# One layer of a gated HGRN2 / Mamba-2 hybrid: thirteen more pairs of projections as Strassen products, in a stage of their own

## The chip, the cores and the metric

The kernel runs on one core of a Trainium2 chip. A core has a matrix engine (PE), a vector engine (DVE), an activation engine (ACT), GpSimd (POOL), and queues on SP and POOL that start transfers between HBM and the on-chip memory. The metric is device microseconds (us) of one execution; shown are the median of several executions and, for one of them, a profile. In the rows L87 is line 87 of the kernel, and `out<-in` names the tiles that an instruction writes and reads.

## The reference, cut to what matters

1024 prompt tokens and 8 single-token samples go through one layer, 1032 columns in all. From the normed input `h` one projection gives everything:

```python
proj = h @ p['w_in']
q, f, i, og, z, xbc, dt, ga, gb = jnp.split(proj, IN_OFFSETS, axis=-1)
...
o_hg, S_new = _hgrn2_recurrence(qh, kh, vh, lh, S_hg)               # 8 heads of 128
o_hg = _rmsnorm(o_hg, p['hg_norm']) * jax.nn.silu(og)               # norm per head, gate og
...
y, h_new = _ssd_recurrence(xh * dtv, la, Bm, Cm, h_ssm)             # 8 groups, 4 heads of 64 each
y = y + p['d_skip'] * xh
y = y * jax.nn.silu(z)                                              # gate z
y = _rmsnorm(y.reshape(Bsz, T, SSM_GROUPS, 256), p['ssm_norm'])     # norm per group
u = jax.nn.sigmoid(ga + bma) * (o_hg @ p['w_br_a']) + jax.nn.sigmoid(gb + bmb) * (y @ p['w_br_b'])
x = x + g1 * (u @ p['w_out'])
x = x + g2 * (jnp.square(jax.nn.relu(h2 @ p['w_up'])) @ p['w_down'])
```

Neither recurrence reads `og`, `z`, `ga` or `gb`; these four enter behind the recurrences.

## The kernel before

Activations lie transposed: a plane is 128 channels by 1032 columns, and `h` is eight planes, each split into a rounded high part and the rest (`hh`, `hl`), as are all weights (`load_w`, L52 to L56). A **dense block** (`dense`, `dense_split`, L87) makes one output plane from eight input planes: three column parts of 344, eight planes, three products high/low, so 72 matmuls of 128x344.

A **Strassen pair** (`strassen_pair`, L1177) makes two output planes at once from halves of the columns and of the inputs: 7 products x 2 quarters x 4 planes x 3 = 168 matmuls of 128x258, in the order 1, 7, 6, 2, 5, 4, 3. It needs sums and differences of the input planes (`strassen_planes`), built once, and of the two weights (`strassen_weights`), built for every pair by ACT (L1133, L1138, L1141, L1145) and DVE (L1123, L1135) into two buffers that are handed on from product to product: the weights of product 1 of the next pair can be made only when product 4 of this one is through, and product 3 runs meanwhile. `keep` and `evac` take the results from the banks. In the kernel before, only `w_up` uses it, for 13 pairs.

The stages follow each other: HGRN2 (`phase_hgrn`; a head has dense blocks for f, i, q, og, and its recurrence follows), two gate blocks, `dt_phase`, eight SSM groups (`ssm_group`: blocks z, z, then B, C, x, x with their convolution, then the recurrence, the gate z and the norm), with the other gate blocks between and behind the groups, then `phase_merge` (`w_br_a`, `w_br_b`), `phase_out`, `phase_ffn`. Gated heads, groups and gate logits go through DRAM (`od`, `yd`, `gd`).

What sets the order: the program is written block after block; a scheduler then orders each engine's instructions, may fill a wait with later work, and prefers what stands under `high_priority`. Beside that, `beside` and `tick` lay a generator's steps between the matmuls of the dense blocks: a `yield n` asks for n matmuls before the next step. HGRN2's recurrence runs this way (`hgrn_head` returns the generator `hgrn_recurrence`); the SSM recurrence is straight code. Each engine works strictly in its order, so one waiting instruction holds all behind it. Weights and most planes are loaded by the SP queue, the stores of `w_up`'s results by the POOL queue.

The norms over channels are column sums on PE: `ones_sum` splits the squares into two parts and multiplies them by a 128x128 matrix of ones (L186, L187), three times for each head and each group; `rstd_from` follows on ACT and DVE over 128 partitions.

## Time and profile before

| | |
|---|---|
| median of 3 runs | 2526.72 us (2524.09 to 2531.59) |
| the profiled execution | 2523.55 us; its span 2521.7 us |
| PE busy | 2482.5 us, 98% |
| DVE, ACT, POOL busy | 1636.7, 1021.3, 70.2 us |
| moved by DMA | 301.14 MB, mean 119 GB/s |
| granted PE clock | 0.995 |

The span goes from the first to the last instruction; the execution's own time is 1.85 us more. A matmul's busy time overlaps with that of the next, so what a stream of matmuls costs is read from the stretch it fills over its count, not from its mean duration. A row of groups ends with the busy time, the mean of one instruction, and the idle time just before them with what ended it. In this execution the HGRN2 heads take 64 us each, to about 587 us; the SSM groups run from about 604 us to 1457 us with their gate blocks, the merge and output stages to 1871 us, the Strassen pairs of `w_up` from 1871 to 2133 us, and `w_down` to the end.

### The profile page before, as it was taken

What the parts mean: (1) busy time and instruction counts of PE and PEld (TensorE: products, weight loads), DVE (VectorE), ACT (ScalarE), POOL (GpSimd) and SP (SyncE); (2) the same over time, 40 slices, a digit from 0 to 9 for tenths busy, and PEclk for the clock granted to TensorE, in tenths of its full rate; (3) what the DMA queues carried; (4) which work ended last, traced back from release to release, by engine and by line L of the source; (5) the groups of instructions that cost most, each with busy time, mean ns of one, the idle gap of its engine ahead of it and who ended that gap; (6) DMA issues with size and microseconds to landing.
All of it is one profiled execution on the core that took longest, in us unless ns stands there. A gap on an engine that the chain in (4) does not pass through costs nothing.

```text
span 2521.7 us, 50588 instructions
## 1 busy us (share of the span) xinstructions
PE 2482.5 (98%) x21486; PEld 2427.6 (96%) x21486; DVE 1636.7 (65%) x3186; ACT 1021.3 (40%) x1569; POOL 70.2 (3%) x138
## 2 busy tenths in 40 slices
PE   8999999999999999999999999999999999999997
PEld 7999999999999999999999999999999999899997
DVE  7566666655677687787887844357976666443356
ACT  4444444445443544535535533124533334221123
POOL 0000000000000000000000000000012222000000
PEclk9999999999999999999999999999999999999999
DMA  6322223333334243243343554224233325232134
GB/s 256 119 103 88 101 103 103 103 105 94 102 111 135 86 145 127 94 146 126 102 145 111 187 188 147 72 102 142 98 108 104 104 101 193 102 110 93 67 106 146
DMA packets 103267, 301.14 MB, mean 119 GB/s; under 512 B 19057, under 2 KB 26033, under 8 KB 103025
## 3 DMA queue, kind: packets, MB, share of 16 engines
q1 hardware_dynamic: 96352, 279.99, 32.8%
q0 software_dynamic: 6256, 17.57, 2.0%
q8 instruction: 168, 2.75, 0.5%
q14 instruction: 59, 0.48, 0.1%
q10 hardware_dynamic: 432, 0.35, 0.0%
HBM read 241.02 MB, written 57.10 MB: 118 GB/s over the span
## 4 chain that ended last, share of the span: by engine, by line
PE 90%; DVE 3%; issue 3%; DMA 2%; ACT 1%; POOL 1%; SPq 0%; DVEq 0%; POOLq 0%; ACTq 0%
PE acc L87 69%; PE b L1177 7%; PE acc L139 2%; PE lv_ps L589 2%; PE y_ps L862 1%; PE yi_ps L866 1%; PE kvx_ps L826 1%; PE o_ps L561 1%; POOL ad L1203 1%; PE kv_ps L543 1%; PE ada_ps L225 1%; PE xt_ps L814 1%; PE cb_ps L796 1%; DMA vb<-vd 1%; DVE wl L56 0%
## 5 line engine op out<-in xcount | busy, mean ns | idle before, releaser
L87 PE MATMUL acc<-hl,wh 128*128 128x344 f32 x2232 | 725.0, 325 | 0.0
L87 PE MATMUL acc<-hh,wl 128*128 128x344 f32 x2232 | 718.3, 322 | 0.0
L87 PE MATMUL acc<-hh,wh 128*128 128x344 f32 x2232 | 715.6, 321 | 0.0
L87 PEld LDWEIGHTS acc<-hl,wh 128*128 128x128 f32 x2232 | 419.4, 188 | 4.3 <-issue 1.4
L87 PEld LDWEIGHTS acc<-hh,wl 128*128 128x128 f32 x2232 | 419.7, 188 | 1.5 <-issue 1.4
L87 PEld LDWEIGHTS acc<-hh,wh 128*128 128x128 f32 x2232 | 419.6, 188 | 0.1
L87 PE MATMUL acc<-hi,wl 128*128 128x344 f32 x1224 | 391.6, 320 | 1.3 <-DVE wl L56 1.3
L87 PE MATMUL acc<-lo,wh 128*128 128x344 f32 x1224 | 391.2, 320 | 1.4 <-ACT wh L54 1.4
L87 PE MATMUL acc<-hi,wh 128*128 128x344 f32 x1224 | 391.2, 320 | 0.0
L56 DVE TENSOR_TENSOR wl<-wr,wh 128x1024 fp32r<-128x1024 f32 x198 | 242.2, 1224 | 203.8 <-ACT wh L54 202.4
L54 ACT ACTIVATE wh<-wr 128x1024 fp32r<-128x1024 f32 x198 | 208.9, 1056 | 397.7 <-PE acc L87 325.7
L87 PEld LDWEIGHTS acc<-hi,wl 128*128 128x128 f32 x1224 | 230.1, 188 | 2.1 <-DVE wl L56 1.9
L87 PEld LDWEIGHTS acc<-lo,wh 128*128 128x128 f32 x1224 | 229.9, 188 | 2.0 <-ACT wh L54 2.0
L87 PEld LDWEIGHTS acc<-hi,wh 128*128 128x128 f32 x1224 | 230.2, 188 | 0.2
L1011 DVE SCALAR_TENSOR_TENSOR x<-acc,modT,x 128x344 f32<-128x344 f32 (+1 forms) x120 | 68.6, 572 | 187.8 <-PE acc L87 187.1
L746 DVE SCALAR_TENSOR_TENSOR cv<-raw,cst,cv 128x1024 f32<-128x1024 f32 x96 | 122.6, 1278 | 0.0
L1177 PE MATMUL b<-tl,wh 128*128 128x258 f32 x416 | 117.6, 283 | 0.0
L1177 PE MATMUL b<-th,wl 128*128 128x258 f32 x416 | 117.6, 283 | 0.0
L1177 PE MATMUL b<-th,wh 128*128 128x258 f32 x416 | 117.5, 283 | 0.0
L1203 POOL DMA_DIRECT2D ad<-r x122 | 65.9, 541 | 1491.5 <-DVE nrm_t L171 1227.8
L738 ACT ACTIVATE raw<-acc 128x344 f32<-128x344 f32 x96 | 43.0, 456 | 120.9 <-PE acc L87 120.4
L1177 PE MATMUL b<-h2h,wh 128*128 128x258 f32 x312 | 88.1, 283 | 0.0
(278 smaller groups left out, 4245.8 us busy)
## 6 DMA issues: line engine op xcount, KB each, us to landing
wr<-w_ssm SPq DMA_DIRECT2D x48, 512.0 KB
wr<-w_down SPq DMA_DIRECT2D x48, 512.0 KB
wr<-w_ada SPq DMA_DIRECT2D x36, 512.0 KB
lo<-ad SPq DMA_DIRECT2D x32, 516.0 KB
wr<-w_hg SPq DMA_DIRECT2D x32, 512.0 KB
w<-cumd SPq DMA_DIRECT2D x32, 512.0 KB
wr<-w_up SPq DMA_DIRECT2D x32, 512.0 KB
ad<-r POOLq DMA_DIRECT2D x104, 129.0 KB, 2.3
```

The source lines that it names most:

```text
L54: nc.scalar.activation(wh, wr, AF.Copy)
L56: nc.vector.tensor_tensor(wl, wr, wh.bitcast(F32), op=ALU.subtract)
L87: last = nc.tensor.matmul(acc[:M, :SW], a[:, sl], b[:, cs(s)], start=(i == 0 and j == 0), stop=(i == n - 1 and j == 2))
L139: k.nc.tensor.matmul(ac[s][:, :SW], a[:, sl], b[:, cs(s)], start=(i == 0 and j == 0), stop=(i == self.n - 1 and j == 2))
L225: nc.tensor.matmul(ps[r, :64], k.scT[:, i, :], w[:, :, r], start=i == 0, stop=i == KD - 1, tile_position=(0, 32 * g))
L543: nc.tensor.matmul(ps[:, c * P:(c + 1) * P], ktok[:, cc], vtok[:, cc], start=True, stop=True)
L589: nc.tensor.matmul(out, QK[hf][:, HT + key:HT + key + 32], x, start=True, stop=True, tile_position=(0, 32 * g))
L738: dense(k, w, k.hX, lambda s, ps: nc.scalar.activation(raw[:, 3 + s * SW:3 + (s + 1) * SW], ps, AF.Copy))
L746: nc.vector.scalar_tensor_tensor(cv[:, :T], raw[:, j:j + T], cw[:, j:j + 1], cv[:, :T], ALU.mult, ALU.add)
L1011: nc.vector.scalar_tensor_tensor(dst[:, :n], ps[:, :n], gate[:, 0:1], base[:, :n], ALU.mult, ALU.add)
L1177: nc.tensor.matmul(acc, a[:, sl], x[:, cols], start=(p in (1, 7, 2) and i == 0 and j == 0), stop=(i == KD // 2 - 1 and j == 2), skip_group ...
L1203: return r, lambda: nc.gpsimd.dma_start(ad[j][:, cols], r)
```

## The change

Blocks og (8), z (16) and two gate logits leave the HGRN2 and SSM stages. Behind the last SSM group a new stage, `phase_late`, builds the sums and differences of `h` while three gate blocks run, then makes 13 Strassen pairs in the order og, z, z, four times, and a pair of gates; one plain gate block ends it. HGRN2 stores its heads ungated and without norm, with the reciprocal root as one row (`rh`); the SSM stores its groups ungated. In the new stage the POOL queue brings them back; beside the next pair they are gated (`og_post`, `z_post`), the group norm is made there and applied one pair later, and POOL stores them again.

Norms: `row_rstd` multiplies the unsplit fp32 squares by 32 columns of ones, the three column parts into three 32-partition strips; the root runs over 96 partitions once; three rows go to DRAM and come back broadcast.

The SSM recurrence becomes a generator laid between the dense blocks of the next group (or the gate blocks) by `beside`. In it the subtraction and clipping in front of the exponential go from DVE (L849) to ACT (`Relu`), and the samples' part of the convolution becomes one instruction instead of three. HGRN2's decode work and the `w_ada` pairs are placed among the steps of the recurrence. `tick` is now also called by `strassen_pair` and `DenseK`.

```diff
-    nc.scalar.activation(a, ss, AF.Identity, bias=k.c_eps, scale=scale)
+    nc.scalar.activation(a, ss, AF.Identity, bias=k.c_eps[:a.shape[0]], scale=scale)
...
-    og = plane("og", "D")
-    dense(k, w[hd * 4 + 1], k.hX, copy_to(og))
-    tables(k, ((og, og, AF.Silu), (q, q, AF.Silu)))
-    return hgrn_recurrence(k, hd, f, F, dec, be, kd8, q, og, st, vb, vtok)
...
+    tables(k, ((q, q, AF.Silu),))
+    return hgrn_recurrence(k, hd, f, F, dec, be, kd8, q, st, vb, vtok)
...
+    nc.sync.dma_start(k.od[hd], o)
+    sq = plane("osq", "D")
+    nc.scalar.activation(sq, o, AF.Square)
+    yield 12
+    row_rstd(k, sq, 1.0 / (P * P), k.rh[hd], [k.sp.tile([P, SW], F32, tag=t, name=t, bufs=b)
+                                            for t, b in (("nrm_a", 1), ("nrm_y", 2), ("nrm_t", 1))])
+
+
+def row_rstd(k, sq, scale, rows, tiles):
+
+    nc = k.nc
+    ps = rec_ps(k, "ss")
     for s in range(NS):
...
+        nc.tensor.matmul(ps[32 * s:32 * s + 32, :SW], k.ones[:, :32], sq[:, cs(s)], start=True, stop=True,
+                         tile_position=(0, 32 * s))
+    y = rstd_from(k, ps[:96, :SW], SW, scale, [t[:96] for t in tiles])
+    nc.gpsimd.dma_start(rows.rearrange("o (s c) -> (o s) c", s=NS), y[0:96:32, :])
...
-    zs = []
-    for a in range(2):
-        z = plane("z", "D")
-        dense(k, w[g * 6 + 4 + a], k.hX, lambda s, ps: nc.scalar.activation(z[:, cs(s)], ps, AF.Copy))
-        zs.append(z)
...
+    return ssm_recurrence(k, g, Bc, Cc, xs)
...
-                    nc.vector.tensor_scalar(W[:, hh, cc], W[:, hh, cc],
-                                            k.tok["cumT"][:, hf * 4 + c, h0 + hh:h0 + hh + 1], 0.0,
-                                            ALU.subtract, ALU.min)
-            nc.scalar.activation(W, W, AF.Exp)
...
+                    nc.scalar.activation(W[hf][:, hh, cc], W[hf][:, hh, cc], AF.Relu, scale=-1.0,
+                                         bias=k.tok["cumT"][:, hf * 4 + c, h0 + hh:h0 + hh + 1])
+            nc.scalar.activation(W[hf], W[hf], AF.Exp, scale=-1.0)
+            yield 12
...
+def late_planes(k, T, i):
+
+    nc = k.nc
+    a, b = [k.pp.tile([P, NT], F32, tag="D", name=n) for n in ("ta", "tb")]
+    for x, (xh, xl) in ((a, k.hX[i]), (b, k.hX[i + 4])):
+        nc.vector.tensor_tensor(x, xh.bitcast(F32), xl.bitcast(F32), op=ALU.add)
+    differences(k, a, b)
+    for x, ts in ((a, (1, 3)), (b, (4, 2))):
+        p = split_plane(k, x, "T", "th", "tl")
...
+    for i in range(KD // 2):
+        late_planes(k, T, i)
+        if i < 3:
+            gate_block(k, next(gates), "D")
+    X = strassen_operands(k.hX, T)
...
+    def og_post(og, j, o, ybc):
+        tables(k, [(og[a], og[a], AF.Silu) for a in (1, 0)])
+        yield 39
+        late()
+        yield 15
+        for a in range(2):
+            nc.vector.scalar_tensor_tensor(o[a], o[a], k.hgn, ybc[a], ALU.mult, ALU.mult)
+            nc.vector.tensor_tensor(o[a], o[a], og[a], op=ALU.mult)
+            nc.gpsimd.dma_start(k.od[2 * j + a], o[a])
+            yield 24
+
+    def z_post(z, g, y):
+        tables(k, [(z[a], z[a], AF.Silu) for a in (1, 0)])
+        yield 39
+        late()
+        yield 15
+        for a in range(2):
+            nc.vector.tensor_tensor(y[a], y[a], z[a], op=ALU.mult)
+            nc.scalar.activation(z[a], y[a], AF.Square)
+            yield 12
+        yield 12
+        nc.vector.tensor_tensor(z[0], z[0], z[1], op=ALU.add)
+        yield 18
+        rows = k.rz[g]
+        row_rstd(k, z[0], 1.0 / 256, rows, [k.sp.tile([P, SW], F32, tag="sq", name="zn", bufs=2) for _ in range(2)]
+                 + [k.sp2.tile([P, SW], F32, tag="mt", name="zt", bufs=2)])
+        nc.gpsimd.dma_start(z[1], rows.broadcast_to([P, NT]))
...
+                i = nc.vector.scalar_tensor_tensor(y[a], y[a], k.ssm_norm[:, pl:pl + 1], z[1], ALU.mult, ALU.mult)
+                order(k, i, k.kept)
+                nc.gpsimd.dma_start(k.yd[pl], y[a])
+        pending.append(apply)
+
+    for n in range(12):
+        if n % 3 == 0:
+            j = n // 3
+            og, o, ybc = planes("D", "og"), planes("E", "o"), planes("E", "ybc")
+            for a in range(2):
+                nc.gpsimd.dma_start(o[a], k.od[2 * j + a])
+                nc.gpsimd.dma_start(ybc[a], k.rh[2 * j + a].broadcast_to([P, NT]))
+            strassen_pair(k, [k.i["w_hg"][(2 * j + a) * 4 + 1] for a in range(2)], X, pair(og))
+            beside(k, og_post(og, j, o, ybc))
+        else:
+            g = n // 3 * 2 + n % 3 - 1
+            z, y = planes("D", "z"), planes("E", "y")
+            for a in range(2):
+                nc.gpsimd.dma_start(y[a], k.yd[2 * g + a])
+            strassen_pair(k, [k.i["w_ssm"][g * 6 + 4 + a] for a in range(2)], X, pair(z))
+            beside(k, z_post(z, g, y))
...
             if g >= 0:
-                if g == 0:
-                    finish(k)
-                    dt_phase(k)
-                ssm_group(k, g)
-            for _ in range((2, 2, 2, 1, 1, 1, 1, 1, 5)[g + 1]):
...
+                beside(k, ssm_group(k, g))
+            for _ in range((3, 0, 1, 0, 1, 0, 1, 0, 4)[g + 1]):
```

Three places show how instructions move. On ACT, from the last matmul of product 4 of one Strassen pair to the weights of products 6 and 2 of the next. Before, between pairs of `w_up` (`wh` are weights, `r` and `s` results):

```order
L1133 ACTIVATE wh<-wr 128x512
L1206 ACTIVATE r<-b_20933 128x258
L1133 ACTIVATE wh<-wr 128x512
L1206 ACTIVATE r<-b_20934 128x258
L1166 ACTIVATE s_21195<-b_21177 128x258
L1138 ACTIVATE wh<-wr 128x1024
```

The change, between the first pair (og) and the second (`L1260` is product 1's and then 7's weights, `L1265` those of 6 and 2):

```order
L1260 ACTIVATE wh<-wr 128x512
L71 ACT_TABLE_LOAD
L71 ACTIVATE og<-og 128x1032
L1135 ACTIVATE og<-b_13280 128x258
L1135 ACTIVATE og<-b_13281 128x258
L1260 ACTIVATE wh<-wr 128x512
L71 ACTIVATE og<-og 128x1032
L75 ACT_TABLE_LOAD
L1265 ACTIVATE wh<-wr 128x1024
```

Two table loads and two gates of 1032 columns now stand between the weights that PE takes next.

On PE, the SSM recurrence's output matmuls (`y_ps`, `yi_ps`) among dense matmuls (`acc`) of the following group. Before:

```order
L862 MATMUL y_ps<-w,xdt 64x128 x8
L866 MATMUL yi_ps<-cv,hs 128x128
L87 MATMUL acc<-hh,wl 128x344
L87 MATMUL acc<-hh,wh 128x344
L87 MATMUL acc<-hl,wh 128x344
L87 MATMUL acc<-hh,wl 128x344
L87 MATMUL acc<-hh,wh 128x344
L87 MATMUL acc<-hl,wh 128x344
L866 MATMUL yi_ps<-cv,hs 128x128
```

The change:

```order
L881 MATMUL y_ps<-w,xdt 64x128 x8
L885 MATMUL yi_ps<-cv,hs 128x128 x3
L87 MATMUL acc<-hl,wh 128x344
L87 MATMUL acc<-hh,wl 128x344
L87 MATMUL acc<-hh,wh 128x344
```

Dense matmuls stood there already; now they come in longer runs and the recurrence's in one piece.

On the POOL queue, which was empty between the SSM and `w_up`, the change's transfers around the second og pair (`yd<-y` stores a group of the first triple, `o`, `ybc` and `y` are loads, `z<-rz` a row broadcast):

```order
L1183 DMA yd_80<-y 128x1032
L1183 DMA yd_81<-y 128x1032
L1191 DMA o<-od_74 128x1032
L1192 DMA ybc<-rh_114 128x1032
L567 DMA rz_121<-zn 3x344
L1191 DMA o<-od_75 128x1032
L1176 DMA z<-rz_121 128x1032
L1158 DMA od_74<-o 128x1032
```

The loads of the og pair stand behind the stores that free their buffers.

More of the change, by code (lines that the diff above doesn't have):

```diff
@@ L513, in hgrn_recurrence @@
         QK.append(t)
-    yield 54
-    yield from scores(k, q, QK, dec)
+    qz = k.qz[hd % 2]
+    nc.vector.tensor_copy(qz[:, :NB], q[:, T:])
+    yield 36
+    od_ps = None
+    for h in SMALL + (32, 64):
+        strips(k, q, QK, h)
+        if h == 2:
+            ada_pair(k, 8 + 2 * hd, ada)
+        elif h == 64:
+            ada_pair(k, 9 + 2 * hd, ada)
+            od_ps = rec_ps(k, "od_ps")
+            for bb in range(NB):
+                g = bb % 4
+                nc.tensor.matmul(od_ps[32 * g:32 * g + 32, bb // 4 * P:(bb // 4 + 1) * P], qz,
+                                 st[:, bb * P:(bb + 1) * P], start=True, stop=True)
+        step(k, QK, dec, h)
+        if h == 1:
+            nc.vector.tensor_tensor(ch(st[:, :T]), ch(st[:, :T]), bc(F[:, T:]), op=ALU.mult)
+        elif h == 4:
+            nc.vector.tensor_tensor(ch(vb[:, :T]), ch(vb[:, :T]), bc(kd8), op=ALU.mult)
+        elif h == 8:
+            ada = ada_load(k, 9 + 2 * hd, [stage(k), stage(k)])
+        elif h == 16:
+            small_scores(k)
+        elif h == 32:
+            nc.vector.tensor_tensor(st[:, :T], st[:, :T], vb[:, :T], op=ALU.add)
+            nc.sync.dma_start(k.o["hg_s"][hd], st[:, :T])
+        yield 16 if h in (1, 4, 16, 32) else 13
+    large_scores(k)
+    os = k.sp.tile([P, 2 * P], F32, tag="os", name="os", bufs=1)
+    nc.scalar.activation(os, od_ps[:, :2 * P], AF.Copy)
     ktok = plane("ktok", "B")
@@ L631, in small, with large_scores @@
             nc.scalar.activation(sT[r, :, r], sc[r].rearrange("p (c i) -> p c i", i=32), AF.Copy)
-    def large(hf):
+def large_scores(k):
+    for hf in range(2):
         sT = ch(k.sT[:, hf * HT:(hf + 1) * HT])
@@ L685, in dt_phase, with dt_rest, plane @@
             nc.vector.tensor_tensor(x[:, cs(s)], x[:, cs(s)], acc[:HS, :SW], op=ALU.add)
+    cw = k.conv_w[:, :, :3].unsqueeze(3).broadcast_to([P, 32, 3, NB])
+    nc.vector.tensor_tensor(k.scv, k.scv, cw, op=ALU.mult)
+    for j in range(2):
+        nc.vector.tensor_tensor(k.scv[:, :, j + 1, :], k.scv[:, :, j + 1, :], k.scv[:, :, j, :], op=ALU.add)
+    nc.vector.tensor_tensor(k.scv[:, :, 2, :], k.scv[:, :, 2, :], k.conv_b.unsqueeze(2).broadcast_to([P, 32, NB]),
+                            op=ALU.add)
+    beside(k, dt_rest(k, x, dt))
+def dt_rest(k, x, dt):
+    nc = k.nc
+    HS = 32
+    late = k.late
+    def plane(name, tag="B"):
+        return k.pp.tile([P, NT], F32, tag=tag, name=name)
     nc.scalar.activation(dt[:, :NT], x[:, :NT], AF.Abs)
@@ L720, in dt_phase @@
                           ddd[:, a, :].unsqueeze(0).broadcast_to([64, HS // 2, 2 * NB]))
+    yield 60
     k.tok = {}
@@ L942, in load_gate @@
     k.sigmoid = k.nc.scalar.activation(t, t, AF.Sigmoid)
+    if after is not None:
+        order(k, k.sigmoid, after)
     return t
@@ L952, in mul @@
         return lambda s, ps: nc.vector.tensor_tensor(u[m][:, cs(s)], u[m][:, cs(s)], ps, op=ALU.mult)
+    raw = [k.pp.tile([P, NT], F32, tag="L", name="or") for _ in range(4)]
+    with k.tc.high_priority(AHEAD):
+        for i in range(4):
+            nc.sync.dma_start(raw[i], k.od[i])
     d = DenseK(k, (k.i["w_br_a"][0], k.i["w_br_a"][1]), (mul(0), mul(1)))
-    u += [load_gate(k, m, "Q1") for m in range(2)]
     oX = []
```

267 lines of the change are left out of this document (133 added, 134 removed).

## The prediction

> **What bounds the kernel now.** I read the page's busy times and slices first, then what PE waited for, then the stretches in which PE does one kind of work only.
>
> ```profile
> PE 2482.5 (98%) x21486; PEld 2427.6 (96%) x21486; DVE 1636.7 (65%) x3186; ACT 1021.3 (40%) x1569; POOL 70.2 (3%) x138
> ...
> PE   8999999999999999999999999999999999999997
> ...
> PEclk9999999999999999999999999999999999999999
> GB/s 256 119 103 88 101 103 103 103 105 94 102 111 135 86 145 127 94 146 126 102 145 111 187 188 147 72 102 142 98 108 104 104 101 193 102 110 93 67 106 146
> ```
>
> The reader is to see that PE is full in every slice at full clock, so time goes down only where PE gets fewer or cheaper instructions, or where one of its few waits goes. Those, longest first in total:
>
> ```profile
> PE acc L139 <- DVE lo L919: 7.5, 3, 4.4
> ...
> PE ss L187 <- DVE sql L183: 3.8, 2, 3.0
> ...
> PE tok_ps L726 <- DVE dd L707: 1.0, 1, 1.0
> ```
>
> The first lies in `w_down`, which stays; the other two belong to steps that go or are laid beside other work. What a matmul costs in a full stream is the stretch over the count; the rows give stretch, PE busy and weight loads with their counts:
>
> ```profile
> 2160.00:2440.00 280.00, 280.00 (x1781) 280.00 (x1780) 1.00 0.25 83
> ...
> 1871.30:2133.30 262.00, 262.00 (x2184) 261.93 (x2184) 1.00 0.34 116
> ```
>
> Above dense matmuls of 344 columns, 280.00/1781 = 0.1572 us; below the 13 Strassen pairs of `w_up`, 262.00/2184 = 0.1200 us, so 20.15 us a pair against 144 x 0.1572 = 22.64 us for two dense blocks.
>
> **The change part by part.** *Strassen.* 26 blocks go, 1872 matmuls x 0.1572 = 294.3 us; 13 pairs come, 2184 x 0.1200 = 262.0 us if they run as in `w_up`. Term: -32.3 us.
>
> *Norms.* Matmul starts in an SSM group (a sum in the stream), and around the fp32 sum of the output stage:
>
> ```profile
> 1129.46 0.32 PE L186 MATMUL ss<-sqh,ones_r 128*128 128x344 f32 x1
> 1129.62 0.32 PE L87 MATMUL acc<-hl,wh 128*128 128x344 f32 x1
> ...
> 1742.93 0.85 PE L1031 MATMUL ss<-sqa,ones_r 128*128 128x344 f32 x2
> 1743.36 0.58 PE L87 MATMUL acc<-uh,wl 128*128 128x344 f32 x1
> 1743.77 0.31 PE L87 MATMUL acc<-uh,wh 128*128 128x344 f32 x1
> ```
>
> An old sum costs 0.16 us; 8 heads and 8 groups x 6 are 96, 15.1 us, and the 3.8 us of waits leave with them. A new one is three fp32 strips of 344 columns; a single full-width one takes 0.43 us (in two passes) and 0.25 us before PE is back at its pace. If the three strips run together, 0.7 us; one after another, 3 x 0.43 + 0.25 = 1.5 us. I take 0.7, since they use different columns of the array; 16 are 11.2 us (upper bound 24). Term: -15.1 - 3.8 + 11.2 = -7.7 us.
>
> *HGRN2 and SSM without their gates.* A head and a group with one gate block, all engines (stretch, then PE, PEld, DVE, ACT, POOL busy):
>
> ```profile
> 270.60:334.60 64.00, 63.92 (x955) 61.11 (x954) 43.00 (x92) 30.93 (x55) 0.00 (x0) 1.00 0.29 102
> ...
> 1072.20:1169.10 96.90, 96.90 (x678) 94.82 (x678) 78.38 (x163) 47.26 (x71) 0.00 (x0) 1.00 0.37 122
> ```
>
> Both are already as long as PE's work, so laying the SSM recurrence beside dense blocks gains nothing by itself: the order shows dense matmuls between its steps before. I count 0 for it. PE's share of a group without gate block falls by three blocks and the sums to 96.9 - 34.0 - 1.0 = 62 us; does DVE fit? Its rows in that group:
>
> ```profile
> L56 DVE TENSOR_TENSOR wl<-wr,wh 128x1024 fp32r<-128x1024 f32 x7 | 8.6, 1223 | 15.4 <-ACT wh L54 15.4
> L849 DVE TENSOR_SCALAR w<-w,cumT 128x128 f32<-128x128 f32 x32 | 7.0, 279 | 0.0
> ...
> L897 DVE SCALAR_TENSOR_TENSOR cv<-cv,cst,nrm_y 128x344 f32<-128x344 f32 x6 | 3.2, 570 | 0.0
> ...
> L748 DVE SCALAR_TENSOR_TENSOR cv<-late,cst,cv 128x8 f32<-128x8 f32 x12 | 2.6, 219 | 0.0
> ...
> L887 DVE TENSOR_TENSOR cv<-cv,z 128x1032 f32<-128x1032 f32 x2 | 2.4, 1224 | 0.0
> ...
> L171 DVE SCALAR_TENSOR_TENSOR nrm_t<-nrm_y 128x344 f32<-128x344 f32 x3 | 1.5, 511 | 0.1
> ```
>
> Gone are 3 of 7 weight splits (3.7), the subtraction (7.0), the norm (3.2 and five rows of 1.5), two thirds of the samples' convolution (1.7) and the gate (2.4): 78.4 - 25.5 = 53 us under 62, about the share of before (78.4 under 96.9). HGRN2 loses a block from DVE's 43.0 as from PE. The `tok_ps` wait goes: -1.0 us. SP's broadcast loads for `w` are issued ahead of the plane's transposes, weight loads behind them; three staging buffers cover that, so 0.
>
> *The new stage.* PE's work there is in the first two terms; the question is which waits come. DVE per pair, rows of the whole run (65, 39, 13 and 78 belong to 13 pairs):
>
> ```profile
> L1123 DVE TENSOR_TENSOR wl<-wr,wh 128x512 fp32r<-128x512 f32 (+1 forms) x65 | 58.6, 901 | 39.4 <-ACT wh L1141 24.6 <-ACT wh L1138 14.3 <-PE b L1177 0.4
> L1123 DVE TENSOR_TENSOR wr<-wr 128x512 f32<-128x512 f32 x39 | 26.9, 689 | 0.9
> L1135 DVE TENSOR_TENSOR wr<-wr 128x512 f32<-128x512 f32 x13 | 8.9, 684 | 0.0
> L1232 DVE TENSOR_TENSOR r<-s,b 128x258 f32<-128x258 f32 x78 | 33.0, 424 | 51.1 <-PE b L1177 51.1
> L746 DVE SCALAR_TENSOR_TENSOR cv<-raw,cst,cv 128x1024 f32<-128x1024 f32 x96 | 122.6, 1278 | 0.0
> ```
>
> Weights 94.4/13 = 7.3, results 33.0/13 = 2.5; a z pair adds 3 x 1.22, three 0.51, and 2 x 1.28 to apply the norm, 7.7: 17.5 of 20.15 us. It fits, but an instruction that is late is late for PE. Two places decide. First ACT between two pairs:
>
> ```profile
> 1173.12 1.28 ACT L71 ACT_TABLE_LOAD   x1
> 1174.41 2.02 ACT L71 ACTIVATE cv<-cv 128x1032 f32<-128x1032 f32 x2
> 1176.45 1.28 ACT L75 ACT_TABLE_LOAD   x1
> 1177.75 0.55 ACT L929 ACTIVATE gate<-acc,cst 128x344 f32<-128x344 f32 x1
> ...
> 2029.65 0.28 PE L1177 MATMUL b<-h2l,wh 128*128 128x258 f32 x1
> ...
> 2029.85 0.63 ACT L1133 ACTIVATE wh<-wr 128x512 fp32r<-128x512 f32 x1 [5.09 <-PE b L1177]
> 2031.27 0.39 ACT L1206 ACTIVATE r<-b 128x258 f32<-128x258 f32 x1 [0.78 <-PE b L1177]
> ...
> 2034.64 1.06 ACT L1138 ACTIVATE wh<-wr 128x1024 fp32r<-128x1024 f32 x1
> ```
>
> Product 3 starts at 2029.65, ACT begins product 1's weights 0.2 us later. From there the new order gives ACT 0.63 + 1.28 + 1.0 (gate) + 2 x 0.36 + 0.63 + 1.0 + 1.28 + 1.06 = 7.6 us until the weights of 6 and 2, DVE's part 1.22 and two handovers of 0.1: ready at 9.0. PE has products 3, 1, 7 and one matmul, 3 x 2.88 + 0.12 - 0.2 = 8.55 us. PE waits about 0.5 us, behind each of 12 gated pairs: +6 us (bounds 0 and, with every step 0.1 us slower, 14).
>
> By the Trainium skill's ScalarE: Activation LUTs, What ACT_TABLE_LOAD costs, a switch is 1283 ns of load and some 1380 ns of drain; that would add 2.76 us to each of 12 boundaries, 33 us. The trace agrees on the load and shows no drain behind it.
>
> A rival takes up such a standstill in rows below. Second, POOL: its transfers by size, median issue to landing:
>
> ```profile
> ad<-r POOLq DMA_DIRECT2D x104, 129.0 KB, 2.3
> ...
> late<-scv POOLq DMA_DIRECT2D x1, 384.0 KB, 3.6
> ...
> L1203 POOL DMA_DIRECT2D ad<-r x122 | 65.9, 541 | 1491.5 <-DVE nrm_t L171 1227.8 <-DVE r L1233 177.0 <-DVE r L1207 83.0
> ```
>
> So a plane of 516 KB takes some 4.3 us. In three of the four og pairs the two stores of `yd` must land before `o` and `ybc` load into their buffers, and DVE's `o*ybc` waits in front of the next pair's first weights. Along DVE's order from the boundary on: the weights of 6 and 2 at 9.0 us, the first application 1.28, a difference 0.69, the weights of 5 and 4 when ACT has them (11.3) 1.22, the second application 1.28, so 13.9 us. Store and load, 8.6 us, end at 22.5. DVE has by then done the group's sum (1.22), five of six results (2.1), product 3's weights (0.7) and the root (1.5), and waited for PE and ACT some 1.7 us in between: it is there at 21.1, and PE has 0.3 us to spare: 1.1 us x 3 = +3 us (bounds 0 and, with transfers of twice that, 16). The other transfers of the stage (24 planes back, 24 stored, 16 rows broadcast, 8 rows stored) are 72 issues of 0.54 us, 39 us of POOL in 270, and stand ahead of what needs them by a pair; the merge behind reads planes stored two pairs earlier or more, so 0. A triple of pairs moves 11.4 MB in 61 us, 187 GB/s, which slices of the page have reached. By the Trainium skill's DMA: Bandwidth & Descriptors, Anatomy of one DMA, an estimate for 516 KB is 3.2 us, with which this wait would vanish; no row here has that size.
>
> The sums of `h` (four times 2 x 1.22, 4 x 0.69, 2 x 1.22, so 31 us of DVE) lie under three gate blocks and what is left of the fourth, 294 matmuls or 46 us, with DVE's other work just in time: +2 us for entry and exit of the stage (0 to 8).
>
> **Sum.** -32.3 - 7.7 - 1.0 + 6 + 3 + 2 = -30 us: 2523.55 - 30 = 2493.5 for the profiled execution. The median of before lies 3.2 us above its profiled execution; with that, **2497 us**.
>
> **Rivals.** *No new waits* (20%): ACT and POOL keep up, as `w_up` does without any PE wait; -41 us, 2486. Against it stands ACT's chain above.
> *The new stage runs on its chains* (8%): DVE is taken for 17.5 of 20.15 us in strict order and every handover is late; pairs of 22.5 us add 13 x 2.35 = 31 us to 2486: 2517 to 2522, no change.
> *A table load holds ACT as long again as it lasts* (2%): 24 x 1.28 = 31 us on 2497, 2528; the 1174.41 row speaks against it.
> *Slower: the SSM's `w`* (7%). ACT takes the subtraction:
>
> ```profile
> L631 ACT ACTIVATE sT<-sTc 32x128 f32<-32x128 f32 x64 | 19.7, 308 | 20.4 <-DVE sTc L626 19.7
> ...
> L852 ACT ACTIVATE w<-w 128x1024 f32<-128x1024 f32 x32 | 33.8, 1055 | 25.7 <-DVE w L849 17.9 <-DMA out_ss_p<-hs 7.8
> ```
>
> Per plane 2 x (8 x 0.31 + 1.06) = 7.1 us on ACT, 1.2 on DVE, before `y_ps`; between a plane's transposes and `y_ps` PE's new order has 48 dense matmuls and the plane's own, some 9 us. Should a pair of `Silu` with its two table loads (4.6 us) fall in between and `w` not be started earlier, PE waits up to 3.9 us for each of 16 planes, 62 us: 2559. It turns to a loss from 30/16 = 1.9 us a plane. Against it: before, DVE's 8 x 0.28 stood in the same place, and no `y_ps` is among PE's waits.
> *The change does not do what it says*: in part so, since the SSM recurrence lay beside dense blocks before; that is in the sum.
>
> **How the numbers follow.** The sum's own case has 63%, range 2487 to 2512 by its bounds. Eight in ten: 2480 (no waits, strips free) to 2520. What a measurement can tell here from no change is 0.3%, 7.6 us, so faster is below 2519: 63 + 20 and 3 of the chain rival, 86%; same 7%; slower 7%.
>
> **What would show it.** Matmuls of 258 columns: 4368 at 0.120 us; fp32 sums at 0.7 us; an ACT or DVE wait of about 0.5 us at the third product of each new pair, a POOL transfer ended just before the `o*ybc` of the og pairs; groups without gate at 62 us, heads at 52 us. It is wrong if PE waits for `w` or `cx` in the SSM, or new pairs take over 21.5 us.

## The result and the profile after

The changed kernel took 2491.74 us (median of four, 2490.75 to 2494.03) beside 2525.4 us for the kernel before (median of four, 2521.56 to 2531.59): a ratio of 0.9866 with a 95% interval of 0.9844 to 0.9887. The profiled execution took 2491.5 us with a span of 2489.7 us, 32.0 us below the span before. The forecast was 2497 us, and for the profiled execution 30 us less; by the medians the change is 33.7 us.

The page, its busy times and the granted clock:

```profile
PE 2446.5 (98%) x21798; PEld 2385.5 (96%) x21798; DVE 1614.4 (65%) x2823; ACT 1090.4 (44%) x1735; POOL 113.4 (5%) x220
...
PEclk9999999999999999999999999999999999999999
```

PE is still the bound, at full clock but for short stretches, with 312 more instructions in less time. The waits of PE that changed, in the same columns as before:

```profile
PE b L1304 <- DVE wl L1250: 8.1, 7, 3.0
...
PE tok_ps L732 <- DVE dtw L707: 0.2, 1, 0.2
```

The first row is new: the Strassen pairs wait for weights, which before they never did. One of its seven is in `w_up`, the others are in the new stage. The wait at `tok_ps` fell from 1.0 to 0.2 us. Next, stretches of the program (length, then busy PE, PEld, DVE, ACT, POOL with counts, granted clock, share of DMA, GB/s): a head, an SSM group without gate block, one with, the new stage, and the 13 pairs of `w_up`:

```profile
125.20:177.80 52.60, 51.85 (x883) 48.96 (x881) 32.29 (x71) 24.49 (x41) 0.58 (x1) 1.00 0.33 114
547.50:609.30 61.80, 61.80 (x456) 59.91 (x455) 55.71 (x93) 38.42 (x68) 0.00 (x0) 1.00 0.43 140
609.30:682.30 73.00, 73.00 (x528) 71.21 (x526) 57.91 (x100) 42.68 (x74) 0.00 (x0) 1.00 0.48 162
1108.72:1390.70 281.98, 274.74 (x2235) 266.38 (x2234) 198.17 (x270) 163.78 (x256) 34.97 (x66) 0.99 0.49 164
1840.36:2102.00 261.64, 260.62 (x2175) 260.41 (x2175) 164.45 (x298) 92.82 (x171) 55.01 (x102) 1.00 0.34 114
```

Heads and SSM groups are where the forecast had them, 52 and 62 us. The new stage is 282.0 us long. Its 2184 matmuls at the pace of `w_up` are 262.0 us, and its eight norm sums 8 x 0.71 = 5.7 us; the other 14.3 us are waits and what comes behind them. The account of the 32 us by kind is taken from the starts of successive matmuls. Each interval is put down to the instruction that begins it, so most of the wait at `tok_ps` lies in the row of the dense blocks:

```
                                   before    after    difference   predicted
dense blocks (tok_ps wait in it)   1829.1   1531.7      -297.4      -294.3, tok_ps -1.0
Strassen pairs                      262.0    539.2      +277.2      +262.0, waits +9, entry and exit +2
group norm sums                      22.1     11.3       -10.8        -7.7
all else                                                  -0.6         0
first to last matmul               2508.3   2476.7       -31.6       -30
```

A norm sum in the stream of matmuls:

```profile
1162.37 0.28 PE L1304 MATMUL b<-th,wh 128*128 128x258 f32 x1
1162.58 0.78 PE L564 MATMUL ss<-z,ones_r 128*32 128x344 f32 x6
1163.29 0.39 PE L1304 MATMUL b<-tl,wh 128*128 128x258 f32 x1
```

Three strips in two passes, six matmuls, take 0.71 us together; the next matmul is 0.23 us before its successor where 0.12 is the pace. By pairs (counted from 0), the places of the stage where two successive matmuls of a product start more than 0.27 us apart are of two kinds. One is product 6: in pairs 1, 2, 3, 6, 9 and 12 its second matmul starts 0.29 to 0.30 us after the first (and 0.20 and 0.21 us in pairs 5 and 11). The other is larger. Product 1 of pairs 4, 7 and 10 waits 0.40, 0.74 and 0.32 us, and product 7 of pairs 5, 8 and 11 waits 1.95, 3.2 and 1.5 us. The largest of these is seen on VectorE's, PE's and POOL's timelines (start, length, and at the end the idle time before and what ended it):

```profile
1278.90 0.69 DVE L1262 TENSOR_TENSOR wr<-wr 128x512 f32<-128x512 f32 x1
1282.80 1.23 DVE L1167 TENSOR_TENSOR y<-y,z 128x1032 f32<-128x1032 f32 x1 [3.21 <-DMA y<-yd]
1283.95 0.68 DVE L1250 TENSOR_TENSOR wl<-wr,wh 128x512 fp32r<-128x512 f32 x1
```

```profile
1284.69 0.58 PE L1304 MATMUL b<-th,wl 128*128 128x258 f32 x1 [3.03 <-DVE wl L1250]
```

```profile
1268.77 0.53 POOL L1183 DMA_DIRECT2D yd<-y  x1 [1.88 <-DVE y L1181]
1269.29 0.53 POOL L1199 DMA_DIRECT2D y<-yd  x1
1275.64 1.05 POOL L1199 DMA_DIRECT2D y<-yd  x2 [5.82 <-DMA yd<-y]
```

DVE is in strict order. It stands at `y*z` for a plane of `y`, and behind it stand the rounded weights of product 7 that PE needs. POOL issued that load only at 1275.64, since the plane it goes to was still being stored from the `y` before, and DVE went on 7.2 us later. In the stage as a whole three loads of `y` waited so for a store of `y`, and three times DVE waited for such a load:

```profile
POOL y L1199 <- DMA yd<-y: 17.2, 3, 5.8
...
DVE y L1167 <- DMA y<-yd: 6.7, 3, 3.2
```

The waits at product 1 look the same, with `o*ybc` in the place of `y*z`; on DVE in front of pair 7:

```profile
1255.95 1.29 DVE L1156 SCALAR_TENSOR_TENSOR o<-o,hgn,ybc 128x1032 f32<-128x1032 f32 x1 [1.86 <-DMA ybc<-rh]
1257.16 0.42 DVE L1137 TENSOR_TENSOR og<-s,b 128x258 f32<-128x258 f32 x1
1257.49 0.68 DVE L1250 TENSOR_TENSOR wl<-wr,wh 128x512 fp32r<-128x512 f32 x1
```

Behind the longest wait PE lost more than the wait. In the stretch behind it the granted clock (the number before the last two) is 0.59 in the mean:

```profile
1285.10:1288.60 3.50, 3.50 (x20) 3.50 (x20) 3.30 (x4) 2.75 (x5) 0.53 (x1) 0.59 0.47 142
```

There 14 matmuls follow each other at 0.21 us in place of 0.12, which is 1.3 us more. So the 14.3 us are 9.3 us of waits (8.1 at products 1 and 7, 1.2 at product 6), 1.6 us for the first intervals behind them, 1.3 us at the lower clock, 1.5 us behind the norm sums, and a small rest.

### The profile page after: what moved, and what is told of

It is laid out like the page before. It is cut to its first block, busy times and chain, and to the rows that moved or that the text cites. A ratio compares the mean times of both kernels' runs of the same rounds, so it can differ in the third digit from the quotient of the medians.

```text
span 2489.7 us, 51129 instructions
## 1 busy us (share of the span) xinstructions
PE 2446.5 (98%) x21798; PEld 2385.5 (96%) x21798; DVE 1614.4 (65%) x2823; ACT 1090.4 (44%) x1735; POOL 113.4 (5%) x220
## 4 chain that ended last, share of the span: by engine, by line
PE 72%; issue 14%; DVE 5%; DMA 4%; ACT 3%; POOL 3%; SPq 0%; POOLq 0%; DVEq 0%; ACTq 0%
PE acc L87 56%; PE b L1304 3%; POOL ad L1331 2%; PE lv_ps L584 2%; PE acc L139 1%; PE y_ps L881 1%; PE yi_ps L885 1%; PE kvx_ps L846 1%; PE o_ps L547 1%; DMA y<-yd 1%; PE kv_ps L529 1%; PE ada_ps L203 1%; PE cb_ps L808 1%; DVE wl L1250 1%; PE xt_ps L833 1%
## 5 line engine op out<-in xcount | busy, mean ns | idle before, releaser
L87 PE MATMUL acc<-hl,wh 128*128 128x344 f32 x1608 | 530.5, 330 | 0.9 <-issue 0.8
L87 PE MATMUL acc<-hh,wh 128*128 128x344 f32 x1608 | 514.9, 320 | 0.0
L87 PE MATMUL acc<-hh,wl 128*128 128x344 f32 x1608 | 514.6, 320 | 0.0
L87 PEld LDWEIGHTS acc<-hh,wh 128*128 128x128 f32 x1608 | 302.1, 188 | 0.0
L1304 PE MATMUL b<-th,wl 128*128 128x258 f32 x832 | 236.8, 285 | 6.3 <-DVE wl L1250 6.1
L1304 PE MATMUL b<-tl,wh 128*128 128x258 f32 x832 | 236.0, 284 | 0.0
L1304 PE MATMUL b<-th,wh 128*128 128x258 f32 x832 | 235.6, 283 | 0.0
L1304 PEld LDWEIGHTS b<-th,wl 128*128 128x128 f32 x832 | 157.9, 190 | 8.4 <-DVE wl L1250 8.1
L1304 PEld LDWEIGHTS b<-tl,wh 128*128 128x128 f32 x832 | 157.9, 190 | 4.5 <-issue 4.5
L1304 PEld LDWEIGHTS b<-th,wh 128*128 128x128 f32 x832 | 158.1, 190 | 0.0
```

Source lines behind the costliest of these rows:

```text
L87: last = nc.tensor.matmul(acc[:M, :SW], a[:, sl], b[:, cs(s)], start=(i == 0 and j == 0), stop=(i == n - 1 and j == 2))
L1304: nc.tensor.matmul(acc, a[:, sl], x[:, cols], start=(p in (1, 7, 2) and i == 0 and j == 0), stop=(i == KD // 2 - 1 and j == 2), skip_group ...
```

## The experiments

The changed kernel was timed again as the mark for the runs beside it; all others are read by their ratio to the kernel before, which ran beside each.

> The changed kernel itself, timed beside the three that follow, as the mark that they are read against. Every theory: 0.9866 of the kernel before, 2491 to 2494 us.

Measured: 2494.76 us, 0.9887 (0.9873 to 0.9901); the stage from its first to its last pair took 260.1 us (260.6 in the first profile), the waits in `b` rows 8.2 us in 7 places. Single waits differ by up to 2.7 us between the two (product 7 of pair 8: 3.2 and 0.5 us), their sum hardly.

### Is the placing of the recurrence worth anything?

```diff
-                beside(k, ssm_group(k, g))
+                rec = ssm_group(k, g)
+                finish(k)
+                for _ in rec:
+                    pass
```

> Only the placing of the SSM recurrence is taken back: its instructions are written as one piece behind the dense blocks of their group, and the scheduler alone places them. Theory of the prediction (placing is worth 0, since TensorE did not wait for the recurrence before or after): within 3 us of the changed kernel. Rival (placing is what makes the SSM groups 61.7 us long): 2 us or more in each of 8 groups, 2508 us or more.

Measured: 2496.81 us, 0.9886 (0.9871 to 0.9901). The recurrence's first matmuls (`cb_ps`) of three groups in turn start at 547.6, 609.7 and 682.6 us, so groups are still 62.0 and 72.9 us. The placing is worth nothing that can be measured, as the prediction had it.

### What are the products worth in this stage?

```diff
-            strassen_pair(k, [k.i["w_ssm"][g * 6 + 4 + a] for a in range(2)], X, pair(z))
+            plain([k.i["w_ssm"][g * 6 + 4 + a] for a in range(2)], z)   # two dense blocks; og and gates likewise
```

> Only the product form is taken back: the 13 pairs of the last stage run as plain dense blocks (1872 matmuls of 344 columns at 0.1572 us, so 294.3 us) in the same place, with the same norms, gates, loads and stores beside them; the Strassen planes are still made. In the changed kernel the stage takes 282.0 us, of which 262 are its matmuls, 5.7 the fp32 sums and 14.3 waits. Theory: the gain of the products is real and partly eaten by waits; with plain blocks the sums stay, and the waits go or stay: from 294.3 + 5.7 - 282.0 = 18 us more than the changed kernel (waits gone) to 32 us more (waits stay). I take 21. Rival (the stage runs on its VectorE and DMA chains, not on TensorE): within 5 us of the changed kernel.

Measured: 2515.3 us, 0.9962 (0.9949 to 0.9974), 20.5 us more than the changed kernel on the same chip. Four blocks of the stage, 288 matmuls and three others:

```profile
1266.90:1312.40 45.50, 45.50 (x291) 45.32 (x288) 16.14 (x15) 21.80 (x29) 5.83 (x11) 1.00 0.50 175
```

PE is busy throughout and has no wait in this stage. DVE is busy for 16.1 of 45.5 us there against 198.2 of 282.0 in the changed kernel. So of the 32.3 us that the products take from PE, 20.5 are left, and 11.8 go into waits, and slower matmuls behind them, which appear only where DVE and ACT have the work of the products as well.

### Where do the larger waits come from?

The planes are given out in another order, `o*ybc` stands later in the program, and `late()`, which applies the norm to the `y` before and stores it, stands 24 matmuls earlier in an HGRN pair's steps:

```diff
-            og, o, ybc = planes("D", "og"), planes("E", "o"), planes("E", "ybc")
+            og, ybc, o = planes("D", "og"), planes("E", "ybc"), planes("E", "o")
...
         tables(k, [(og[a], og[a], AF.Silu) for a in (1, 0)])
-        yield 39
+        yield 15
         late()
-        yield 15
+        yield 75
```

> Only the order in which planes are reused in the last stage changes: ybc is given its two planes ahead of o, so that the next y takes planes that are read out early and does not wait for the store of o; and the product o*ybc of an HGRN gate pair stands 75 ticks behind the last y, where it stood 15. Work and DMA bytes are the same. Theory A (TensorE's waits at product 7 of pairs 5, 8 and 11, 1.95 + 3.2 + 1.5 us, and at product 1 of pairs 4, 7 and 10, 0.4 + 0.7 + 0.3 us, come from loads on POOL's queue that stand behind a store whose plane they need): those six waits go, 8 us less than the changed kernel, 2484 us. Theory B (they come from the time of a load itself, some 7 us from issue to use with two under way): the waits move by a few us of a pair but stay, within 2 us of the changed kernel.

Measured: 2490.12 us, 0.9860 (0.9847 to 0.9874), 4.6 us less than the changed kernel on the same chip, but hardly less than its first ratio, 0.9866; the stage from first to last pair took 256.8 us, 3.3 us less. The three waits at product 7 are gone: the loads of `y` now wait at most 1.8 us for a store of `y`, where it was up to 5.8. Whether the other planes did that or the earlier store is not told apart here. The waits at product 1 stayed (0.4, 0.7 and 1.4 us), and 0.9 us came at product 6 of pairs 4, 7 and 10. From the list of the stage's waits (total, times, longest), from DVE's timeline at the end of the third HGRN pair, and from POOL's before it:

```profile
DVE o L1156 <- DMA ybc<-rh: 11.8, 5, 2.8
```

```profile
1254.65 1.29 DVE L1156 SCALAR_TENSOR_TENSOR o<-o,hgn,ybc 128x1032 f32<-128x1032 f32 x1 [1.81 <-DMA ybc<-rh]
1255.87 0.41 DVE L1137 TENSOR_TENSOR og<-s,b 128x258 f32<-128x258 f32 x1
```

```profile
1250.48 0.53 POOL L1192 DMA_DIRECT2D ybc<-rh  x1 [2.70 <-DMA yd<-y]
```

No row of DVE shows a wait for `y<-yd` any more. But `o*ybc`, written 90 ticks into the next pair, is executed before the last result of its own pair: it needs only `o` and `ybc`, and the scheduler put it ahead of that result. DVE then stands 1.81 us for the load, which POOL issued 4.2 us before. Theory A got 3 to 5 of its 8 us; that the time of the loads themselves has a part, as theory B had it, is not excluded.

The tables were taken away in another run, with the Silu:

```diff
-        tables(k, [(z[a], z[a], AF.Silu) for a in (1, 0)])
+        for a in (1, 0):
+            with k.tc.high_priority(AHEAD):
+                nc.scalar.activation(z[a], z[a], AF.Copy)      # og likewise
```

> The two table loads of 1.28 us between pairs of the last stage are taken away: the Silu of z and of the HGRN output gates is left out, and a plain copy of the same planes stands in its place (same sizes, no table change). In the changed kernel TensorE shows a step of 0.30 instead of 0.12 us inside product 6 of pairs 1, 2, 3, 6, 9 and 12, behind these loads. Theory: the ACT term of the prediction is real but small; the step falls to 0.12 us in those pairs and the kernel gets 1 to 3.5 us shorter. Rival (the prediction's ACT term of 0.5 us in each of 12 pairs, some of it inside the larger waits): 6 us shorter. Rival (each table load holds ACT for a further 1.3 us that no row shows): 10 us or more shorter, with ACT's idle time between the loads and what follows them gone.

Measured: 2493.18 us, 0.9868 (0.9851 to 0.9884), 1.6 us below the mark on another chip, so no difference. The step at product 6 is gone: pair 1 takes 20.16 us where it took 20.45. But the stage from first to last pair takes 261.0 us, because the scheduler has laid out DVE in another order, and PE waits in other places:

```profile
PE b L1308 <- DVE og L1137: 4.7, 3, 2.2
PE b L1308 <- DVE wl L1254: 3.6, 4, 1.0
PE b L1308 <- DVE z L1137: 3.3, 3, 1.7
```

```profile
1255.31 1.29 DVE L1158 SCALAR_TENSOR_TENSOR o<-o,hgn,ybc 128x1032 f32<-128x1032 f32 x1 [6.38 <-DMA ybc<-rh]
1256.52 0.42 DVE L1137 TENSOR_TENSOR og<-s,b 128x258 f32<-128x258 f32 x1
```

Here `o*ybc` came ahead of a result (`og`) that PE waits for, and stood 6.38 us for its load. The tables cost about 0.3 us a pair; that the rest of the waits comes from the loads fits these rows, but this run does not show it of each.

ScalarE's order alone, with the weights of products 6 and 2 (`k.w62`) ahead of the second Silu:

```diff
         for out, in_, func in acts:
             i = k.nc.scalar.activation(out, in_, func)
             if prev is not None:
                 order(k, i, prev)
+                if then is not None:
+                    order(k, i, then)                     # then = k.w62
```

> Only ScalarE's order between pairs of the last stage changes: the rounded weights of products 6 and 2 go ahead of the second Silu and of the table load behind it, with the same work. Theory: as for the run without table loads, the step inside product 6 falls to 0.12 us in pairs 1, 2, 3, 6, 9 and 12 and the waits at products 1 and 7 stay: 1 to 3 us shorter than the changed kernel. Rival (TensorE's wait there comes from VectorE's part of these weights): no difference.

Measured: 2499.0 us, 0.9894 (0.9879 to 0.9909), 4 us above the mark, with intervals that overlap, where 1 to 3 us less were expected; the stage from first to last pair took 265.8 us, 5.7 us longer than in the mark. ACT and PE in pair 2:

```profile
1153.78 1.05 ACT L71 ACTIVATE z<-z 128x1032 f32<-128x1032 f32 x1
1154.85 1.28 ACT L77 ACT_TABLE_LOAD   x1
1156.15 1.06 ACT L1270 ACTIVATE wh<-wr 128x1024 fp32r<-128x1024 f32 x1
1157.11 1.20 ACT L1295 ACTIVATE s<-b 128x258 f32<-128x258 f32 x4
```

```profile
1157.53 0.39 PE L1306 MATMUL b<-tl,wh 128*128 128x258 f32 x1 [0.34 <-ACT s L1295]
```

The step at the second matmul of product 6 is gone. Half a product later PE waits for `s`, the copy of product 1's result that product 6 adds onto, which now stands behind the Silu, the load and the next weights. ACT has no gap from 1152.47 to 1159.27 there: what is put ahead pushes something else behind, and the copies had less time to spare than the weights.

Both edits together, with `o*ybc` held behind the copies (`order(k, i, k.kept)`); the steps of an HGRN pair are placed as in the run with the planes in another order:

> The freed planes of the run before it (ybc ahead of o), the product o*ybc also held back until the first three products of its pair are through, and the weights of products 6 and 2 ahead of the second Silu. With the freed planes alone TensorE still waited 5.6 us in 7 places of the last stage (1.0 us at product 6 of pairs 4, 7 and 10, 0.4 to 1.4 us at their product 1), where VectorE stood at o*ybc for the load of ybc. Theory (all waits of the stage are VectorE standing at a product for a late load, or ScalarE at the tables): the stage falls from 282.0 us to 262 + 5.7 and 1 to 3 more, 12 us shorter than the changed kernel, about 0.982 of the kernel before. Rival (a load that comes earlier only moves the wait to the next product of the three): 5 us shorter, as with the freed planes alone.

Measured: 2499.16 us, 0.9894 (0.9879 to 0.9909); 264.8 us from first to last pair. A miss by 16 us: PE waited for `s` 4.0 us in 8 places, and for `wl` 6.7 us in 8.

Next the plane `ybc` was left out, with `o` in its place, and then the Silu as well:

```diff
-            og, o, ybc = planes("D", "og"), planes("E", "o"), planes("E", "ybc")
+            og, o = planes("D", "og"), planes("E", "o")
...
-                nc.gpsimd.dma_start(ybc[a], k.rh[2 * j + a].broadcast_to([P, NT]))
...
-            beside(k, og_post(og, j, o, ybc))
+            beside(k, og_post(og, j, o, o))
```

> The plane ybc of an HGRN gate pair and its two loads are left out, and o stands in its place in the product, so the HGRN group norm's factor is left out of the result; the same VectorE work remains. This frees two planes in each three pairs, and no load of the last stage has to wait for a store. Theory (the waits at products 1 and 7 are VectorE standing at a product for loads that wait for a plane): both kinds go, the small step at product 6 stays: the stage from its first to its last pair falls from 260.5 us (1108.72 to 1369.33) to 251, 9 us shorter than the changed kernel, 2484 us. Rival (the stage has a sum of waits that only moves, as the runs with other orders suggest: VectorE and ScalarE have too much to do about the change from one pair to the next): 0 to 3 us shorter.

> As the run without ybc, and the Silu of z and of the HGRN output gates left out as well (a copy in its place), so that the last stage has neither loads that wait for a plane nor table loads. Theory (two causes, loads and tables, and no third): only the sums remain, the stage from first to last pair takes 12 pairs of 20.15 us and 8 sums of 0.95, 249.4 us, 11 us shorter than the changed kernel, 2481 us. Rival (waits only move): 5 us or less.

Measured: 2487.78 us, 0.9842 (0.9829 to 0.9856) without `ybc`, and 2492.5 us, 0.9862 (0.9849 to 0.9876) without both; 256.1 and 259.7 us from first to last pair. In the first the waits at product 7 of pairs 5, 8 and 11 are gone and those at product 1 of pairs 4, 7 and 10 are larger (0.8 to 1.3 us), with 0.5 us at their product 7. DVE at the end of the third HGRN pair without `ybc` (without both it stands 3.86 us there):

```profile
1252.93 1.29 DVE L1156 SCALAR_TENSOR_TENSOR o<-o,hgn 128x1032 f32<-128x1032 f32 x1 [3.94 <-DMA o<-od]
```

Even without `ybc`, `o` takes the planes of a `y` that is stored in the same pair, and is late. So this edit did not take the cause away, as its expectation had said it would: the order of the pairs leaves `o` waiting for a store. The second run, 4.7 us above the first, lost more than the missing tables gave; its waits lie where those of the other run without tables did.

Then `o*ybc` was held where a stand should do no harm:

```diff
+            i = nc.vector.scalar_tensor_tensor(o[a], o[a], k.hgn, ybc[a], ALU.mult, ALU.mult)
+            order(k, i, k.last)          # the last result read out by VectorE; ybc has its planes ahead of o
...
-        yield 15
+        yield 66                         # between late() and the product
```

> All of the computation, no work left out: ybc gets its planes ahead of o as in the run with freed planes, the last y stays where the changed kernel has it (39 ticks into a pair, so behind the weights of products 6 and 2), and each product o*ybc is held by order behind the evictions of product 2 and of product 5 of its pair, where VectorE may stand for a late load without a weight behind it. Theory (it is VectorE's order, not the amount of its work, that makes TensorE wait): the waits at products 1 and 7 go, 8 to 10 us shorter than the changed kernel, 2483 us, 3 us below the run with freed planes. Rival (the stand at o*ybc then delays the weights of the next pair): as the run with freed planes or above it.

Measured: 2510.87 us, 0.9937 (0.9924 to 0.9949): a miss by 28 us, the rival's way; 277.1 us from first to last pair. DVE and POOL about the third HGRN pair's products:

```profile
1290.91 1.29 DVE L1156 SCALAR_TENSOR_TENSOR o<-o,hgn,ybc 128x1032 f32<-128x1032 f32 x1 [6.50 <-DMA ybc<-rh]
```

```profile
1282.86 0.54 POOL L1193 DMA_DIRECT2D ybc<-rh  x1 [3.71 <-DMA yd<-y]
1283.38 0.53 POOL L1200 DMA_DIRECT2D y<-yd  x1
1283.90 0.54 POOL L1159 DMA_DIRECT2D od<-o  x1
1292.50 0.53 POOL L1200 DMA_DIRECT2D y<-yd  x1 [8.06 <-DVE o L1156]
```

The later product frees its planes later, the loads of `y` that need them come later, and with a load and a store issued right behind it `ybc` takes 8.1 us from issue to use. DVE's stand of 6.5 us reaches past the boundary, and PE waits 2.6 to 5.0 us at product 1 of pairs 5, 8 and 11. In three stretches about these waits the granted clock is 0.50 again, and the matmuls there cost some 4.8 us more. A product moved in time moves the wait with it, because its planes come free later.

### Another order of the pairs

If the shortage comes from `o`, `ybc` and `y` of three pairs taking turns on four planes, then an order in which they do not mix should end it: four HGRN pairs first, then eight pairs of `z`, where `y` takes the planes of the `y` of two pairs before. `o*ybc` is also held behind copies of its pair.

```diff
-    for n in range(12):
+    for n in (0, 3, 6, 9, 1, 2, 4, 5, 7, 8, 10, 11):
...
+            i = nc.vector.scalar_tensor_tensor(o[a], o[a], k.hgn, ybc[a], ALU.mult, ALU.mult)
+            order(k, i, k.kept)
```

> All of the computation, no work left out: the order of the pairs in the last stage changes, the four pairs of HGRN output gates first and the eight pairs of z behind them, where the changed kernel has them as one and two, three and so on. So y takes the planes of the y of two pairs before, and never those of o. The product o*ybc is held by order behind the second product of its pair. Theory (the stage has four planes for o, ybc and y, and TensorE's larger waits are VectorE standing at a product whose load waited for one of them): the waits at products 1 and 7 go, the step at product 6 stays, 8 to 10 us shorter than the changed kernel, 2483 us; in the HGRN pairs, with four loads each, up to 1 us of wait per pair may be left. Rival (a wait of the stage only moves when its order is changed): 3 us shorter to 15 us longer.

Measured: 2482.45 us (2482.27 to 2483.81), 0.9835 (0.9821 to 0.9848). It beats both kernels: its slowest execution is faster than the fastest of the changed kernel (2490.75), and its time lies within 1 us of the forecast. The same stage, 13 pairs:

```profile
1108.63:1380.50 271.87, 271.60 (x2228) 263.64 (x2227) 197.52 (x270) 163.60 (x256) 34.99 (x66) 1.00 0.50 169
```

DVE, ACT and POOL do what they did (197.5, 163.6 and 35.0 us, against 198.2, 163.8 and 35.0), in 10.1 us less. No wait at product 1 or 7 is left, DVE waits for no transfer in the stage, and the granted clock stays at 1.00. But the loads still wait for planes that are being stored:

```profile
POOL y L1200 <- DMA yd<-y: 21.8, 7, 3.9
POOL ybc L1193 <- DMA od<-o: 18.8, 3, 6.7
```

They land before DVE comes to them, and in less time: the median from issue to landing is 4.9 us for `y` and 4.8 for `ybc`, where the changed kernel has 6.3 and 5.9. So what the order took away is the late arrival, not the sharing of planes. How much of it is the order of pairs, the held `o*ybc` or the quicker transfers was not run apart. What is left is the step at product 6. DVE and PE in pair 8:

```profile
1277.42 1.23 DVE L1168 TENSOR_TENSOR y<-y,z 128x1032 f32<-128x1032 f32 x1
1279.33 1.22 DVE L1251 TENSOR_TENSOR wl<-wr,wh 128x1024 fp32r<-128x1024 f32 x1 [0.69 <-ACT wh L1266]
```

```profile
1280.32 0.28 PE L1305 MATMUL b<-tl,wh 128*128 128x258 f32 x1
1280.61 0.39 PE L1305 MATMUL b<-th,wl 128*128 128x258 f32 x1
```

DVE waits 0.69 us for ACT's part of the weights of products 6 and 2, ends at 1280.55, and PE goes on at 1280.61. An ungated pair takes 20.10 us in this kernel, a pair behind gates 20.44 and one with a norm sum too 21.3, so the two table loads and gates cost 0.34 us a pair and a sum 0.9.

### Did VectorE need the relief in the SSM?

```diff
-                    nc.scalar.activation(W[hf][:, hh, cc], W[hf][:, hh, cc], AF.Relu, scale=-1.0,
-                                         bias=k.tok["cumT"][:, hf * 4 + c, h0 + hh:h0 + hh + 1])
+                    nc.vector.tensor_scalar(W[hf][:, hh, cc], W[hf][:, hh, cc],
+                                            k.tok["cumT"][:, hf * 4 + c, h0 + hh:h0 + hh + 1], 0.0,
+                                            ALU.subtract, ALU.min)
-            nc.scalar.activation(W[hf], W[hf], AF.Exp, scale=-1.0)
+            nc.scalar.activation(W[hf], W[hf], AF.Exp)
```

> Only the subtraction that makes the SSM's weights w is put back from ScalarE to VectorE (as one subtract and minimum), everything else as changed. Theory of the prediction: VectorE is busy for some 53 of 62 us of an SSM group without gate and would come to about 60 of 62, so that TensorE begins to wait for VectorE in places: 0 to 20 us longer than the changed kernel; I take 8. Rival (VectorE has room, moving w to ScalarE was worth nothing): within 2 us. Rival (w on ScalarE is itself what holds the groups at 61.7 us): shorter than the changed kernel by 3 us or more.

Measured: 2495.22 us, 0.9875 (0.986 to 0.989), no difference, where I took 8 us more. A group without gate block and one with:

```profile
549.80:611.60 61.80, 61.80 (x457) 59.98 (x456) 56.14 (x102) 26.20 (x34) 0.00 (x0) 1.00 0.41 131
611.60:684.70 73.10, 73.10 (x528) 71.16 (x527) 67.86 (x150) 34.17 (x44) 0.00 (x0) 1.00 0.52 169
```

The 10.4 us of DVE's work that came back for the two groups lie in the second stretch. DVE is busy for 124.0 of 134.9 us, and PE still waits for nothing. Moving `w` to ScalarE was worth nothing, and cost nothing either.

## Why the prediction was right, and which of its terms were not

**Strassen, -32.3 us.** Right in its pace: a pair without gates before it takes 20.1 us in the new stage as in `w_up`. The run with plain blocks gives what was left of it, 20.5 us.

**Norms, -7.7 us.** The strips run together, 0.71 us, as taken. The restart behind a sum was left out: a pair with a sum is 0.9 us longer, so 16 sums cost some 14 us, by an estimate from these eight, where the term has 11.2. The sums that went were worth more: 22.1 us from matmul start to matmul start where the term has 15.1 + 3.8. Together -10.8 by the account, some 3 us of it given back in the restarts that the account puts under the matmuls behind the sums.

**ACT between pairs, +6 us.** The mechanism is shown: the wait is at the second matmul of product 6, behind DVE's part of weights that ACT made late (the last rows above), and goes with the tables. The size was off: 0.3 us a pair where 0.5 was worked out, in pairs where no other wait covers it; with the pairs in the other order all 12 show it, some 4 us with the restarts. A chain of some 9 us was reckoned to within 0.2 us. On the Trainium skill's ScalarE: Activation LUTs, What ACT_TABLE_LOAD costs, which adds some 1380 ns of drain to a load, the trace decides against a drain here:

```profile
1276.49 1.28 ACT L71 ACT_TABLE_LOAD   x1
1277.78 1.07 ACT L71 ACTIVATE z<-z 128x1032 f32<-128x1032 f32 x1
```

The load starts as the instruction before it ends (1275.84 and 0.64 us long), and the Silu as the load ends. With two drains of 1.38 us the weights would be 2.76 us later and PE's step with them; the step is 0.3 us.

**POOL, +3 us.** This is the term that was mis-sized, and its place was half right. The stand at `o*ybc` ahead of the weights of product 1 was foreseen; PE lost 0.40, 0.74 and 0.32 us there, half of 3.3. The stand one step on, at `y*z` ahead of the weights of product 7, was not: there PE lost 6.6 us. The prediction followed the plane from the store of `yd` to `ybc`, and said of the other transfers that they stand ahead of what needs them by a pair. But the loads of `y` too must wait for a store, in the three places that count for one of `y`. And 4.3 us for a plane holds where little is beside it: 4.2 us in one row above, 7.2 us in another, where a second load and a store were issued within 1.2 us. Of the largest wait, 3.2 us, either an earlier issue or a load of 4.2 us would have taken nearly all, so the runs do not settle which of the two weighs more. In all 8.1 us in place of 3; ACT's term and this one were 9 together and are 9.3 in waits alone, 12.2 with the restarts and the lower clock behind them, for which no term stood.

**Entry and exit, +2 us.** Nothing is seen of them: the pairs begin with no wait of PE, pair 0 takes 20.11 us and pair 1 no more than pairs 2 and 3 without their sum.

**The recurrence, 0, and the SSM.** Right, by the run without placing and by the group lengths. DVE's 53 of 62 us in a group are 55.7. The rival of `w` on ScalarE did not come: PE waits for no `w`, and with `w` back on VectorE the time is the same.

**The rivals.** That the stage runs on its chains is refuted by the run with plain blocks, 20.5 us longer, and by the kernel with the other order of pairs, which does the same work in 10 us less. That a table load holds ACT as long again is refuted by the two rows above. No new waits at all would have been 2486; the best order came to 2482.45.

The sum, -30 us, came out as -32.0, and its errors, in the account from first to last matmul (-31.6), partly cancelled. On the one side the stage has 14.3 us beyond its matmuls and sums where the terms have 9 and 2, and `w_up` a wait of about 1 us. On the other side the sums gave 3 us more than their term and the dense blocks 2 us more, which the account does not explain further, and all else 0.6 us. That the total comes so close is in part luck.

## What to carry to other kernels

When loads and stores take turns on a few buffers, follow each buffer to its next owner through a whole period, not only to the load that looks late: the wait that was foreseen was the smaller one. When a wait only moves as one order after another is tried, as it did in most of the kernels here, ask what is short, and change who shares it. An engine at 70% with strict order can hold up one at 98%, and a scheduler may put the instruction that stands for a load ahead of one that another engine needs. Two edits in one run leave open which of them worked.
